# A hybrid retention, attention and RWKV block in float32: RWKV's merge on the preparation's PSUM bank

## The chip, the core and the metric

The kernel runs on one core of one Trainium2 chip. The metric is the device time of one execution in microseconds (us); three executions of the kernel before gave 2938.15, 2952.78 and 2946.3 us, median 2946.3. The engines are named as in the profile: PE is TensorE (matmuls), PEld its weight load, DVE is VectorE, ACT is ScalarE, POOL is GpSimd, SP is SyncE, which issues the DMAs here.

## The reference

Two layers work on 256 latent tokens and 256 context tokens of width 1024. Each layer is half a SwiGLU, a token mixing, and half a SwiGLU. The mixing has three branches that share one input projection: a bidirectional retention, a windowed attention, and a bidirectional RWKV-7. The change touches RWKV alone. For each of its 8 heads (64 wide) and each direction it runs

```
def rwkv7_scan(r, w, k, a, v, kk, s0, reverse):
    '''S_t = S_{t-1} (diag(w_t) - kk_t^T (a_t * kk_t)) + v_t^T k_t ;  y_t = S_t r_t.'''
    def step(S, inp):
        r_t, w_t, k_t, a_t, v_t, kk_t = inp
        sa = -jnp.einsum('bhvk,bhk->bhv', S, kk_t)
        S = (S * w_t[:, :, None, :] + sa[..., None] * (kk_t * a_t)[:, :, None, :]
             + v_t[..., None] * k_t[:, :, None, :])
        return S, jnp.einsum('bhvk,bhk->bhv', S, r_t)
```

over the context from a zero state, and then over the latent tokens from the state that the context left. In the second layer the context's outputs are not wanted, only its states.

## The kernel before, in words

A layer's dense products (`dense`, L346, by way of `mm3`, L185) are split float32: one product is three matmuls (L186, L187, L188) from a high and a low half of the weights and of the activations. Weights stream in by SP (`Weights.get`, L100): a load `raw` (L113), a cast on ACT to `whi` (L114), a subtraction on DVE to `wlo` (L115). In this document a dense matmul means one of these.

RWKV's scan is computed in chunks of 64 tokens, four to a segment (context s = 0, latent s = 1), for a pair of heads p = 0 to 3. Each p has these parts, named by the words of the table `ORDER`:

- `c` (`rw_cols`, L844): r, k and v of the pair, their convolution, the normalised kk.
- `A` and `C` (`rw_prep`, L901, for s = 0 and s = 1), the preparation: decays (L908, L909 and their tanh), scans, the scaled keys `kb`, their transposes `kbT` (L957), the chunk products `gk` and `tg` (L976 and what evacuates them, L980 to L987). All its matmuls go through the PSUM tag `rf`, which has one bank, so each group of matmuls waits until the group before it has been evacuated. At its end the two diagonal 32x32 blocks of each triangular matrix go by DMA through a DRAM tile (L997, L1001) to POOL, which inverts them in 62 instructions (L1008, L1009) and stores the inverse in the DRAM tile `td` (L1012).
- `B` and `D` (`rw_back`, L1146, for s = 0 and s = 1), the back: `rw_merge` (L1015) loads the inverse from `td` into `z` (L1018), transposes it on DVE (L1023) and builds the off-diagonal blocks with 32 small matmuls (L1035, L1040); `rw_vals` (L1045) forms the values `ve` and `vbd` (L1052 to L1060) and, where outputs are wanted, `bv` (L1064); `rw_chain` (L1072) is the walk over the four chunks in both directions, eight steps of L1079, L1081, L1086, L1090 and L1107 with ACT and DVE work between them; `rw_out` (L1117, L1134) normalises the result.

The merge, the values, the walk and the output all go through the PSUM tag `rx`, which has two banks. The walk of `D` starts from the state that the walk of `B` of the same p left.

The order on each engine is not written by hand. The framework's scheduler lays the program out ahead of time with its own estimate of durations: it takes an instruction when what it reads is ready and a home for what it writes is free, and the least urgent dense matmuls fill the places between. So the number of homes of a tag, and which tags share one, set the order on all engines. On the chip each engine then runs its list in that order, whatever the durations turn out to be.

Tags that the change names: `rb` (3 homes) holds the merge's `tn` and `xm`, the walk's `ya` and the output's square; `rt` (8 homes) holds the preparation's temporaries; `ve` (2) the values, `vbd` (one, in the constants' tile `cst`) the values by head; `lo` (3) the low-rank columns of the whole layer.

Of the kernel before, what the change touches and what calls it, by code (L numbers as in the profile page):

```python
# [18 lines left out]
CONSTS = {"ident": 0, "nw": 128, "adab": 176, "ones": 320, "bones": 384, "cm": 512, "mg": 640, "ks": 896, "all": 960}  # L19
# [103 lines left out]
def body(nc, tc, I, O, es, dbg=None):  # L123
# [3 lines left out]
    V, A, G, PE, SP = nc.vector, nc.scalar, nc.gpsimd, nc.tensor, nc.sync  # L127

    def mk(shape, tag, bufs=1, dt=F32):
        return sb.tile(shape, dt, name=tag, tag=tag, bufs=bufs)  # L130
# [3 lines left out]
    def ps(tag):  # L134
        return pp.tile([128, 512], F32, name="ps_" + tag, tag=tag, bufs=NB[tag])
# [13 lines left out]
    def span(S):  # L149
        return slice(S[0] * 256, S[-1] * 256 + 256)  # L150


    cst = mk([128, CONSTS["all"] + 1696 + 4360], "cst")
    n0 = CONSTS["bones"]
    SP.dma_start(out=cst[:, 0:n0], in_=I["cst"][:, 0:n0])
    SP.dma_start(out=cst[:, n0:CONSTS["all"]], in_=I["cst"][:, n0:])
# [1 line left out]
    def const(name, n):  # L158
        return cst[:, CONSTS[name]:CONSTS[name] + n]
# [4 lines left out]
    per = cst[:, CONSTS["all"]:]  # L164
# [3 lines left out]
    def sm(n, key, bufs=8):  # L168

        if key not in rings:  # L170
            rings[key] = [rings["at"], 0, n]
            rings["at"] += n * bufs
            assert rings["at"] <= CONSTS["all"] + 1696 + 4360
        r = rings[key]
        assert r[2] == n
        j = r[0] + n * (r[1] % bufs)
        r[1] += 1
        return cst[:, j:j + n]
# [1 line left out]
    hall = mk([128, KT, 2, 512], "hall", 1, F32R)  # L180
    hs = [(hall[:, kt, 0], hall[:, kt, 1]) for kt in range(KT)]

    rings = {"at": CONSTS["all"] + 1696}

    def mm3(o, w, h, start, stop):  # L185
        PE.matmul(o, w[0], h[0], start=start, stop=False)  # L186
# [19 lines left out]
    st = {"apart": False}  # L206
# [120 lines left out]
    def hl(h, c):  # L327
        return h[0][:, c], h[1][:, c]
# [21 lines left out]
    def first(W, key, H, cs, os, lead=0, lag=0):  # L350

        bl, n = W.take(key), len(os)
        w = {}
        parts = [(0, slice(0, 512))] if lead == 0 else [(0, CS[0]), (lead, CS[1])]
        for i in range(KT + lead + lag):
            for d, part in parts:
                k = i - d
                for j, (o, c) in enumerate(zip(os, cs)):
                    p = slice(max(c.start, part.start), min(c.stop, part.stop))
                    if 0 <= k < KT and p.start < p.stop:  # L360
                        if (k, j) not in w:
                            w[k, j] = W.get(bl[k * n + j])
                        for q in range(2):
                            PE.matmul(o[:, p], w[k, j][q], hl(H[k], p)[0], start=(k == 0 and q == 0 and p.start == c.start), stop=False)  # L364
                k -= lag
                for j, (o, c) in enumerate(zip(os, cs)):
                    p = slice(max(c.start, part.start), min(c.stop, part.stop))
                    if 0 <= k < KT and p.start < p.stop:
                        PE.matmul(o[:, p], w[k, j][0], hl(H[k], p)[1], start=False, stop=(k == KT - 1 and p.stop == c.stop))
# [424 lines left out]
    def conv(o, ct, c, st, dst):  # L794
        w = st["vec"][:, ct * 3:ct * 3 + 3]
        A.activation(dst[:, c], o[:, c], AF.Copy, scale=w[:, 1:2])
        n = (c.stop - c.start) // 256
        d = dst[:, c].rearrange("p (s t) -> p s t", s=n)
        s = o[:, c].rearrange("p (s t) -> p s t", s=n)
        V.scalar_tensor_tensor(d[:, :, 1:256], s[:, :, 0:255], w[:, 0:1], d[:, :, 1:256], ALU.mult, ALU.add)  # L800
        V.scalar_tensor_tensor(d[:, :, 0:255], s[:, :, 1:256], w[:, 2:3], d[:, :, 0:255], ALU.mult, ALU.add)  # L801

    def rw_consts():
        V.memset(per[:, 288:1312], 0.0)
        ub = per[:, 288:800].rearrange("p (d b x) -> p d b x", d=2, b=2)
        return dict(bones=const("bones", 128), cm=const("cm", 128), mg=const("mg", 256).rearrange("p (d x) -> p d x", d=2),
                    one=const("ones", 64), ks=const("ks", 1), ub=[[ub[:, d, b] for b in range(2)] for d in range(2)],
                    vbd=per[:, 800:1312].rearrange("p (q x) -> p q x", q=4))

    def rw_lora(W, H, l, S, st):  # L810
        full = slice(0, 512)
        vec = st["vec"]
        lo = []
        cs, os = (full, full, span(S)), [ps(t) for t in ("mm", "mm", "ap")]
        first(W, "lo", H, cs, os, 1, 1)
        for j, (c, o) in enumerate(zip(cs, os)):
            t = mk([128, 512], "lo", 3)
            conv(o, 12 + j, c, st, t)
            lo.append(t)
        c = span(S)  # L820
        A.activation(lo[0], lo[0], AF.Tanh)
        A.activation(lo[2][:, c], lo[2][:, c], AF.Tanh, scale=0.5)
        V.tensor_scalar(lo[2][:, c], lo[2][:, c], 0.5, 0.5, ALU.mult, ALU.add)
        st["sg"] = lo[2]
        st["lw"] = [[mk([128, 512], "lw", 4, F32R) for d in range(2)] for x in range(2)]
        for x in range(2):
            for d in range(2):
                hs, ot = (slice(64 * y, 64 * y + 64) for y in (d, 1 - d))
                A.copy(st["lw"][x][d][hs], lo[x][hs])
                V.tensor_sub(st["lw"][x][d][ot], lo[x][hs], st["lw"][x][d][hs].bitcast(F32))  # L830
        if l > 0:
            bl = W.take("vd")
            o = ps("mm")
            wh, wl = W.get(bl[0], 2)
            for kt in range(KT):
                ksl = slice(kt * 32, kt * 32 + 32)
                mm3(o[0:32], (wh[:, ksl], wl[:, ksl]), hl(H[kt], full), kt == 0, kt == KT - 1)
            vd = mk([128, 512], "vd")[0:32]
            A.copy(vd, o[0:32])
            st["vd"] = vd  # L840
# [172 lines left out]
        X["td"] = td  # L1013

    def rw_merge(X, st):  # L1015
        z, tn, xm = mk([64, 2, 8, 32], "z", 2), mk([32, 16, 32], "rb", 3)[:, 0:8], mk([64, 16, 32], "rb", 3)[:, 0:8]
        for b in range(2):
            mark = SP.dma_start(out=z[32 * b:32 * b + 32].rearrange("p d u t -> p (d u) t"), in_=X["td"][16 * b:16 * b + 16].rearrange("u j g i -> (j g) u i")).ins  # L1018
        st["marks"].append(mark)
        fl = lambda t: t.rearrange("p u t -> p (u t)")  # L1020
        tg = X["tg"]
        tu = [tg[d].rearrange("p h c t -> p (h c) t") for d in range(2)]
        V.transpose(fl(tn), fl(z[0:32, 0]))  # L1023
        for b in range(2):
            bs = slice(32 * b, 32 * b + 32)
            A.copy(tu[0][bs, :, bs], z[bs, 0])
            V.transpose(tu[1][bs, :, bs], z[bs, 1])

        o = ps("rx")
        ov, o2 = (o[:, j * 256:j * 256 + 256].rearrange("p (u x) -> p u x", x=32) for j in range(2))  # L1030
        ab = (slice(0, 32), slice(32, 64))
        for d in range(2):
            a, b = ab[d], ab[1 - d]
            for u in range(8):
                PE.matmul(ov[b, u], X["off"][a, u], tn[:, u] if d == 0 else z[a, 1, u], start=True, stop=True)  # L1035
        A.copy(xm, ov[0:64])
        for d in range(2):
            a, b = ab[d], ab[1 - d]
            for u in range(8):
                PE.matmul(o2[a, u], xm[b, u], tu[d][b, u, b], start=True, stop=True)  # L1040
        V.tensor_copy(tu[0][ab[0], :, ab[1]], o2[ab[0]])
        A.copy(tu[1][ab[1], :, ab[0]], o2[ab[1]])

    def rw_vals(s, R, st, want_y, X):
        c = CS[s]  # L1045
        v = R["v"]

        ve = [mk([128, 4, 128], "ve", 2) for _ in range(2)]
        vb = st["vbd"]
        o = ps("rx")  # L1050
        for q in range(2):
            PE.matmul(o[:, q * 128:q * 128 + 128], v[:, c.start + q * 128:c.start + q * 128 + 128], st["cm"], start=True, stop=True)  # L1052
        ov = o[:, 0:256].rearrange("p (c d) -> p c d", c=2)
        for a in range(2):
            rows = slice(64 * a, 64 * a + 64)
            for d in range(2):
                A.copy(ve[d][0:64, a::2], ov[rows])
            for h in range(2):
                hs = slice(64 * h, 64 * h + 64)
                A.copy(vb[hs, a::2, hs], ov[rows, :, hs])  # L1060
        X["ve"], X["vb"] = ve, vb
        if want_y:
            o = ps("rx")
            PE.matmul(o[:, 0:256], st["bones"], X["t"][:, 0], start=True, stop=True)  # L1064
            bv = sm(256, "bv", 2)
            V.tensor_tensor(bv, o[:, 0:256], v[:, c], ALU.mult)
            X["bv"] = bv
# [159 lines left out]
    for l in range(2):  # L1227
# [17 lines left out]
        if not RC:  # L1245
            RC.update(rw_consts())
# [120 lines left out]
```

## Time and profile before

| | us |
|---|---|
| median of three runs | 2946.3 |
| the profiled execution | 2950.47 |
| its span, first to last instruction | 2948.7 |
| the mixing of layer 0 (407.8 to 1320) | 912.2 |
| the mixing of layer 1 (2066 to 2758) | 692.0 |
| PE busy in the span | 2797.0 |
| POOL busy in the span | 376.2 |

The profiled execution is 4.2 us over the median of the runs. Busy time is time in which an engine has an instruction under way; a share of it is an average over stages with different limits. In the two mixings RWKV, retention, attention and the dense products are interleaved. The rest of the span is the feed-forward parts, in which the change touches nothing.

### The profile page before, as it was taken

The numbers are of one execution on the slowest core, as the hardware profiler recorded it, in microseconds if no ns is written. First come the engines' busy times: TensorE is split into PE (matmuls) and PEld (weight loads), VectorE is DVE, ScalarE is ACT, GpSimd is POOL, SyncE is SP. The second block draws the span as 40 slices with busy tenths as digits, with TensorE's granted clock in tenths as the row PEclk, the third lists the DMA queues.
The fourth block names the chain that finished last, engine by engine and source line by source line (L and its number), as shares of the span: only waits on it lengthen the run. The fifth ranks groups of instructions, "written<-read, shape, count | busy, mean of one in ns | idle before, by whom it ended". The sixth has DMA issues, their size and how long they took to land. (4 is left out here: it accounts for less than half of the span.)

```text
span 2948.7 us, 47410 instructions
## 1 busy us (share of the span) xinstructions
PE 2797.0 (95%) x16761; PEld 2389.1 (81%) x16761; DVE 2002.5 (68%) x4677; ACT 1319.8 (45%) x2968; POOL 376.2 (13%) x1068
## 2 busy tenths in 40 slices
PE   7999999889999999999999999999989889899999
PEld 6888888767877787788888888888878788788999
DVE  7977668676676666566756466465787767678655
ACT  3322245556555654333223232233567665565544
POOL 0000000522132112000000000000033434330000
PEclk9999999789999999999999999999999888899999
DMA  7655534212333136534534435343433234246554
GB/s 267 232 189 183 163 122 130 83 39 82 111 97 89 49 123 207 176 102 147 195 114 169 147 111 185 104 164 122 137 90 108 75 110 116 61 124 212 170 179 154
DMA packets 259727, 400.97 MB, mean 136 GB/s; under 512 B 78752, under 2 KB 96288, under 8 KB 259488
## 3 DMA queue, kind: packets, MB, share of 16 engines
q1 hardware_dynamic: 259488, 397.93, 42.2%
q8 instruction: 132, 2.16, 0.3%
q14 instruction: 107, 0.88, 0.1%
HBM read 368.33 MB, written 25.82 MB: 134 GB/s over the span
## 5 line engine op out<-in xcount | busy, mean ns | idle before, releaser
L114 ACT CAST whi<-raw 128x512 fp32r<-128x512 f32 x954 | 564.1, 618 | 675.7 <-PE ps_mm L187 350.0
L186 PE MATMUL ps_mm<-hall,whi 128*128 128x512 f32 (+1 forms) x2320 | 845.1, 365 | 10.2 <-DVE rr_v L801 4.0
L188 PE MATMUL ps_mm<-hall,wlo 128*128 128x512 f32 (+1 forms) x2320 | 842.6, 364 | 2.0 <-DVE wlo L115 2.0
L187 PE MATMUL ps_mm<-hall,whi 128*128 128x512 f32 (+1 forms) x2320 | 840.8, 363 | 0.0
L115 DVE TENSOR_TENSOR wlo<-raw,whi 128x512 fp32r<-128x512 f32 x954 | 643.8, 691 | 104.3 <-ACT whi L114 68.3
L186 PEld LDWEIGHTS ps_mm<-hall,whi 128*128 128x128 f32 x2320 | 442.9, 191 | 80.6 <-ACT cst L981 4.4
L188 PEld LDWEIGHTS ps_mm<-hall,wlo 128*128 128x128 f32 x2320 | 441.6, 191 | 74.8 <-DVE wlo L115 4.1
L187 PEld LDWEIGHTS ps_mm<-hall,whi 128*128 128x128 f32 x2320 | 442.0, 191 | 71.4 <-issue 0.2
L186 PE MATMUL ps_mm<-hid,whi 128*128 128x512 f32 (+1 forms) x737 | 260.6, 354 | 0.0
L187 PE MATMUL ps_mm<-hid,whi 128*128 128x512 f32 (+1 forms) x737 | 259.9, 354 | 0.0
L188 PE MATMUL ps_mm<-hid,wlo 128*128 128x512 f32 (+1 forms) x737 | 257.3, 354 | 0.0
L1008 POOL TENSOR_TENSOR cst<-acc,cst 128x60 f32<-128x60 f32 (+24 forms) x496 | 172.4, 348 | 615.5 <-DMA acc<-ad__10934 59.2
L401 DVE TENSOR_TENSOR ft<-ft,ps_mm 128x512 f32<-128x512 f32 (+1 forms) x80 | 49.7, 621 | 210.4 <-PE ps_mm L188 198.1
L373 DVE SCALAR_TENSOR_TENSOR x<-ps_mm,cst,x 128x256 f32<-128x256 f32 x136 | 61.0, 480 | 193.1 <-PE ps_mm L188 193.1
L853 POOL TENSOR_TENSOR ll<-lora,lh 128x512 fp32r<-128x512 f32 x8 | 10.3, 1282 | 1359.2 <-DVE ft L300 942.6
L1009 POOL TENSOR_TENSOR cst<-cst 128x60 f32<-128x60 f32 (+24 forms) x496 | 176.2, 355 | 38.1
L236 DVE SCALAR_TENSOR_TENSOR ft<-m,cd 128x1024 bf16<-128x1024 f32 x136 | 163.0, 1221 | 9.8 <-DMA m<-ada 9.8
L237 DVE SCALAR_TENSOR_TENSOR m<-m,cd 128x1024 f32<-128x1024 f32 x136 | 165.4, 1221 | 0.7
L186 PEld LDWEIGHTS ps_mm<-hid,whi 128*128 128x128 f32 x737 | 139.1, 189 | 19.6
L187 PEld LDWEIGHTS ps_mm<-hid,whi 128*128 128x128 f32 x737 | 139.1, 189 | 19.4
L188 PEld LDWEIGHTS ps_mm<-hid,wlo 128*128 128x128 f32 x737 | 138.5, 189 | 19.4
L187 PE MATMUL ps_mm<-wlo,hall 128*128 128x256 f32 x416 | 122.6, 295 | 2.7 <-DVE wlo L115 2.6
(339 smaller groups left out, 4505.3 us busy)
## 6 DMA issues: line engine op xcount, KB each, us to landing
m<-ada SPq DMA_DIRECT2D x136, 512.0 KB, 4.4
raw<-w0b SPq DMA_DIRECT2D x214, 256.0 KB, 2.9
raw<-w1b SPq DMA_DIRECT2D x211, 256.0 KB, 3.2
raw<-w0a SPq DMA_DIRECT2D x132, 256.0 KB, 2.8
raw<-w0c SPq DMA_DIRECT2D x132, 256.0 KB, 4.5
raw<-w1a SPq DMA_DIRECT2D x132, 256.0 KB, 4.3
raw<-w1c SPq DMA_DIRECT2D x132, 256.0 KB, 3.9
gd<-ft SPq DMA_DIRECT2D x24, 256.0 KB, 2.0
```

What stands on the lines that cost most here:

```text
L114: nc.scalar.copy(hi, raw)
L115: nc.vector.tensor_sub(lo, raw, hi.bitcast(F32))
L186: PE.matmul(o, w[0], h[0], start=start, stop=False)
L187: PE.matmul(o, w[0], h[1], start=False, stop=False)
L188: PE.matmul(o, w[1], h[0], start=False, stop=stop)
L236: V.scalar_tensor_tensor(junk, raw, 1.0, st["cond"][0], ALU.mult, ALU.mult, accum_out=md[:, kt, 0:1])
L237: V.scalar_tensor_tensor(raw, raw, 1.0, st["cond"][1], ALU.mult, ALU.mult, accum_out=md[:, kt, 1:2])
L373: V.scalar_tensor_tensor(xs[n][:, CS[s]], o[:, CS[s]], gate[:, n, s:s + 1], xs[n][:, CS[s]], ALU.mult, ALU.add)
L401: V.tensor_tensor(sg[:, c], sg[:, c], pu[:, c], ALU.mult)
L853: G.tensor_sub(ll, lw, lh.bitcast(F32))
L1008: G.tensor_tensor(w, acc[j // 16][:, j % 16, j + 1:32].unsqueeze(1).to_broadcast([128, m, n]), tt[:, 0:m, j:j + 1].to_broadcast([128, m, n ...
L1009: G.tensor_tensor(tt[:, 0:m, j + 1:32], tt[:, 0:m, j + 1:32], w, ALU.add)
```

## The change

Four things move. The merge's product tile `o` is taken from `rf` (the preparation's one bank) and no longer from `rx` (the walk's two). The merge's tiles `tn` and `xm` are taken from `rt` (8 homes) and no longer from `rb`. `vbd` has a home for each segment, and its zeros cost one more memset. `ve` has four homes, which it shares with the first two low-rank columns; the third keeps `lo`, with one home. The number and the shapes of the matmuls stay as they were.

```
-    cst = mk([128, CONSTS["all"] + 1696 + 4360], "cst")
+    cst = mk([128, CONSTS["all"] + 2208 + 4360], "cst")
...
     def rw_consts():
         V.memset(per[:, 288:1312], 0.0)
+        V.memset(per[:, 1696:2208], 0.0)
...
-                    vbd=per[:, 800:1312].rearrange("p (q x) -> p q x", q=4))
+                    vbd=[per[:, a:a + 512].rearrange("p (q x) -> p q x", q=4) for a in (800, 1696)])
...
-            t = mk([128, 512], "lo", 3)
+            t = mk([128, 512], "ve", 4) if j < 2 else mk([128, 512], "lo")
...
     def rw_merge(X, st):
-        z, tn, xm = mk([64, 2, 8, 32], "z", 2), mk([32, 16, 32], "rb", 3)[:, 0:8], mk([64, 16, 32], "rb", 3)[:, 0:8]
+        z, tn, xm = mk([64, 2, 8, 32], "z", 2), mk([32, 16, 32], "rt", 8)[:, 0:8], mk([64, 16, 32], "rt", 8)[:, 0:8]
...
-        o = ps("rx")
+        o = ps("rf")
...
-        ve = [mk([128, 4, 128], "ve", 2) for _ in range(2)]
-        vb = st["vbd"]
+        ve = [mk([128, 4, 128], "ve", 4) for _ in range(2)]
+        vb = st["vbd"][s]
```

The scheduler lays the program out anew from these, so the order changes on every engine from the first mixing on. In the listings below, lines of the changed kernel stand one higher than before (L1036 is the merge's L1035, L958 the transposes of L957, L977 the products of L976), and equal instructions that follow each other share a row.

PE, layer 1, head pair 1: the preparation's transposes into `ps_rf` (`A1`) in the kernel before. `ps_mm` is a dense product, L1040 a merge.

```order
L1052 MATMUL ps_rx<-cst,rr_v 128x128 x2
L186 MATMUL ps_mm<-whi,hall 128x256
L187 MATMUL ps_mm<-wlo,hall 128x256
L957 MATMUL ps_rf<-cst,kb 128x128 x2
L1040 MATMUL ps_rx<-tg,rb 32x32 x16
L957 MATMUL ps_rf<-cst,kb 128x128 x2
L188 MATMUL ps_mm<-whi,hall 128x256
```

The same preparation in the changed kernel, among steps of the walk `D0` (L1080 to L1108) and retention's scores (L548, L549).

```order
L958 MATMUL ps_rf<-cst,kb 128x128 x4
L548 MATMUL ps_sc<-rqh,rks 128x256
L549 MATMUL ps_sc<-rql,rks 128x256
L958 MATMUL ps_rf<-cst,kb 128x128 x4
L1108 MATMUL ps_rx<-ve,tg 64x64 x4
L977 MATMUL ps_rf<-arz,kb 128x2x64 x2
L1080 MATMUL ps_rx<-cst,gk 128x128
L1082 MATMUL ps_rx<-cst,ar 128x128
L1080 MATMUL ps_rx<-cst,gk 128x128
L1082 MATMUL ps_rx<-cst,ar 128x128
L573 MATMUL ps_po<-cst,ft 128x128 x2
```

The transposes stood among dense matmuls that did not depend on them; now they stand in a stretch without dense matmuls, and the merge of the pair before has moved ahead of the whole preparation.

PE, layer 0, the last merge (`D3`) in the kernel before: L1134 and L1135 are the output of the walk `B3`.

```order
L188 MATMUL ps_mm<-ro,wlo 128x512
L1134 MATMUL ps_rx<-cst,rb 128x64 x4
L1135 MATMUL ps_rx<-lo,cst 128x256
L1035 MATMUL ps_rx<-rb,cst 32x32 x8
L1035 MATMUL ps_rx<-z,cst 32x32 x8
L186 MATMUL ps_mm<-ro,whi 128x512
```

The same merge in the changed kernel, L1036 and L1041, between the L1087 and the L1091 of one step of the walk `B3`.

```order
L1087 MATMUL ps_rx<-cst,tg 64x64 x2
L1036 MATMUL ps_rf<-rt,cst 32x32 x8
L1036 MATMUL ps_rf<-z,cst 32x32 x8
L1087 MATMUL ps_rx<-cst,tg 64x64 x2
L1091 MATMUL ps_rx<-ve,kbT 128x128
L1041 MATMUL ps_rf<-tg,rt 32x32 x16
L186 MATMUL ps_mm<-ro,whi 128x512 x2
L1108 MATMUL ps_rx<-ve,tg 64x64 x2
```

The merge stood directly behind the output of the walk before; now it stands inside that walk, and the rest of the walk is queued behind it.

## Rows read from the trace of the kernel before

**Rows 1.** The page: span, and busy us (share of the span) xinstructions by engine.

```profile
span 2948.7 us, 47410 instructions
PE 2797.0 (95%) x16761; PEld 2389.1 (81%) x16761; DVE 2002.5 (68%) x4677; ACT 1319.8 (45%) x2968; POOL 376.2 (13%) x1068
```

**Rows 2.** Windows: stretch, us, busy (xcount) by engine, granted clock, DMA share, GB/s.

```profile
407.80:1320.00 912.20, 850.07 (x5197) 706.59 (x5196) 624.64 (x1650) 470.05 (x1140) 183.84 (x532) 0.95 0.35 107
1320.00:2066.00 746.00, 740.49 (x3532) 616.97 (x3531) 454.86 (x846) 223.32 (x396) 0.00 (x0) 0.99 0.43 144
2066.00:2758.00 692.00, 626.73 (x4705) 554.52 (x4705) 513.15 (x1385) 415.74 (x1044) 192.15 (x532) 0.92 0.39 116
```

**Rows 3.** Groups on PE: busy us, mean ns | idle us before them <- releaser.

```profile
L976 PE MATMUL ps_rf<-arz,kb 128*128 128x256 f32 (+1 forms) x256 | 69.3, 398 | 2.0 <-DVE tg L987 1.4 <-DVE gk L984 0.3 <-ACT cst L1095 0.3
L1086 PE MATMUL ps_rx<-cst,tg 64*64 64x64 f32 x512 | 54.8, 236 | 6.5 <-ACT cst L1083 6.4
L1079 PE MATMUL ps_rx<-cst,gk 128*128 128x128 f32 (+1 forms) x256 | 54.7, 299 | 12.6 <-DVE cst L1102 6.1 <-DVE rb L1113 5.0 <-ACT tg L1042 0.7
L1090 PE MATMUL ps_rx<-ve,kbT 128*128 128x128 f32 x224 | 44.4, 300 | 3.2 <-ACT ve L1088 2.8
L1107 PE MATMUL ps_rx<-ve,tg 64*64 64x64 f32 x384 | 42.0, 237 | 12.9 <-ACT ve L1088 8.3 <-DVE cst L1102 4.3
L957 PE MATMUL ps_rf<-cst,kb 128*128 128x128 f32 x128 | 24.3, 315 | 9.2 <-DVE kb L946 6.2 <-ACT kbT L958 3.1
L1052 PE MATMUL ps_rx<-cst,rr_v 128*128 128x128 f32 x64 | 13.1, 335 | 2.8 <-ACT kbT L958 2.8
L1035 PE MATMUL ps_rx<-rb,cst 32*32 32x32 f32 x256 | 12.0, 199 | 10.4 <-DVE rb L1023 10.3
L1134 PE MATMUL ps_rx<-cst,rb 64*128 64x64 f32 x48 | 5.6, 238 | 5.7 <-DVE rb L1131 5.7
```

**Rows 4.** Timeline of PE, the first merge: start us, us, instruction, [idle before].

```profile
548.42 0.28 PE L186 MATMUL ps_mm<-whi,hall 128*128 128x256 f32 x1
548.54 0.28 PE L187 MATMUL ps_mm<-wlo,hall 128*128 128x256 f32 x1
...
549.48 1.03 PE L976 MATMUL ps_rf<-arz,kb 128*128 128x256 f32 x4
558.08 0.90 PE L1035 MATMUL ps_rx<-rb,cst 32*32 32x32 f32 x13 [7.57 <-DVE rb L1023]
...
568.16 0.42 PE L187 MATMUL ps_mm<-wlo,hall 128*128 128x256 f32 x1
568.38 0.41 PE L188 MATMUL ps_mm<-whi,hall 128*128 128x256 f32 x1
```

**Rows 5.** Windows, behind that wait.

```profile
553.30:577.10 23.80, 18.42 (x129) 16.91 (x130) 12.43 (x51) 10.04 (x33) 8.01 (x25) 0.50 0.36 98
```

**Rows 6.** Timeline, from the preparation C3 of layer 1 to its merge.

```profile
2606.75 1.03 PE L976 MATMUL ps_rf<-arz,kb 128*128 128x256 f32 x4
...
2616.91 0.24 POOL L1008 TENSOR_TENSOR cst<-acc,cst 128x31 f32<-128x31 f32 x1 [31.75 <-DMA acc<-ad__25540]
...
2644.22 2.54 SPq L1012 DMA_DIRECT2D td<-cst  x4
...
2648.17 0.88 SPq L1018 DMA_DIRECT2D z<-td  x2
...
2652.06 0.59 PE L1035 MATMUL ps_rx<-rb,cst 32*32 32x32 f32 x13
```

**Rows 7.** Timeline of PE, from the preparation C2 of layer 0 to its merge.

```profile
913.61 1.02 PE L976 MATMUL ps_rf<-arz,kb 128*128 128x256 f32 x4
...
995.63 0.46 PE L1134 MATMUL ps_rx<-cst,rb 64*128 64x64 f32 x4
996.65 0.68 PE L1035 MATMUL ps_rx<-rb,cst 32*32 32x32 f32 x13
```

**Rows 8.** Groups on DVE, the memset of the constants.

```profile
L804 DVE MEMSET cst<- 128x1024 f32 x1 | 0.9, 912 | 1.0 <-PEq L1359 1.0
```

More of the change, by code (lines that the diff above doesn't have):

```diff
@@ L172, in sm @@
             rings["at"] += n * bufs
-            assert rings["at"] <= CONSTS["all"] + 1696 + 4360
+            assert rings["at"] <= CONSTS["all"] + 2208 + 4360
         r = rings[key]
@@ L181, in body @@
     hs = [(hall[:, kt, 0], hall[:, kt, 1]) for kt in range(KT)]
-    rings = {"at": CONSTS["all"] + 1696}
+    rings = {"at": CONSTS["all"] + 2208}
     def mm3(o, w, h, start, stop):
```

## The prediction

> **What bounds the kernel now.** I read the page's busy times first: PE is busy 2797.0 of 2948.7 us [rows 1], so a change that leaves PE's work alone can win or lose only where PE stands idle or runs slowly. Then the windows by stage: the feed-forward stretch between the two mixings is busy 740.5 of 746.0 us at a granted clock of 0.99, while the mixings are busy 850.1 of 912.2 and 626.7 of 692.0 at 0.95 and 0.92 [rows 2]. The mixings hold 62.1 + 65.3 = 127.4 us of idle, and of clock 0.05 of 912.2 and 0.08 of 692.0, about 101 us more. Every term below is a share of these.
>
> Then the groups on PE, for what it waits for there. The RWKV groups wait 10.4 us at the merge (L1035), 9.2 + 2.0 = 11.2 in the preparation (L957, L976), 2.8 at the values (L1052), 6.5 + 12.6 + 3.2 + 12.9 = 35.2 in the walk (L1086, L1079, L1090, L1107) and 5.7 at the output (L1134) [rows 3], 65.3 together. The releasers are ACT and DVE, the engines between two dependent groups of matmuls, and none is a bank that comes free late.
>
> The timeline shows what one such wait is. PE issues its list in order: after the first preparation's last L976 it stood 7.57 us before the first merge, with dense matmuls queued behind it [rows 4]. Behind that wait the granted clock was 0.50 for 23.8 us [rows 5], the lower level, 1.2 GHz: dense matmuls of 256 columns that had started 0.12 us apart now started 0.22 apart [rows 4].
>
> Last, the latency under that wait. From the end of a preparation's last L976 (2606.75 + 1.03) to its merge (2652.06) 44.3 us passed [rows 6]: DMAs to POOL's tiles until 2616.91, POOL's 62 instructions until the store at 2644.22, the load of `z`, the transpose. In the six pairs in which the merge came soonest it took 43 to 49 us. So a merge that stands less than about 43 us of PE work behind its preparation makes PE wait, unless other waits on the way fill the time.
>
> **The change part by part.** No matmul is added or removed and no shape changes. What is added is one memset of 128x512 on DVE: the one of 128x1024 took 0.912 us at the program's start, while the inputs were still on their way [rows 8], so this is some 0.46 us, hidden; at worst 0.46. More homes for `ve` and `vbd` let the values be formed ahead of the merge; nothing waits for that by itself, so nothing by itself, and what it gives the walk is in the walk's term. `tn` and `xm` in `rt` take two of eight homes for the few us of a merge; the bound is one wait of the preparation's size, already in its term.
>
> What costs is the order. The merge now takes turns with the preparation in the one bank of `rf`, and the scheduler has moved the preparations late: the transposes of layer 1's A1, which stood among dense matmuls, now stand in a stretch without any, together with the walk of D0. And the merge is no longer behind the previous output but inside the previous walk, as with D3 of layer 0, where the rest of that walk is queued behind it.
>
> How much shorter the cover has become I counted over both built orders. For each pair of dependent groups on PE I added up the PE instructions that stand between them, each at its median distance from start to start in this trace (0.12 us for a dense matmul of 256 columns [rows 4], twice that for 512), and took what is missing to the latency that the same kind of pair has in this trace, taken at the shortest tenth of its pairs (43.3 us from preparation to merge). What is missing in all pairs, before and now:
>
> - preparation to merge: 66 and 88 us (nine short merges of sixteen before, ten now);
> - within the preparation: 33 and 67;
> - values and merge to the walk's first use: 8.3 and 29.6;
> - within the walk: 43.4 and 47.6;
> - walk to output: 13.1 and 18.1.
>
> These are not times, since pairs overlap: 66 us missing at the merges went with 10.4 us of idle there. So I scale each measured idle time with its count. The merge gains 10.4 x 0.33 = 3.5 us, the preparation 11.2 x 1.03 = 11.5, the values 2.8 x 2.57 = 7.2, the walk 35.2 x 0.10 = 3.4, the output 5.7 x 0.38 = 2.2: 27.8 us. With each latency at its shortest pair and not at the shortest tenth the growth is 0.36, 0.91, 3.41, -0.40 and 1.04, and the sum 3.7 + 10.2 + 9.6 - 13.9 + 5.9 = 15.5 us. I take 22 us, between the two. The walk is the term on which they differ: its true bound is -14 to +3.4.
>
> The clock is the unknown. In the mixings 127.4 us of idle went with 101 us of clock, 0.79 us for each, so 22 us more idle may bring 0 to 17 us. I take 0: the wait that cost most, 7.57 us with 23.8 us at 1.2 GHz behind it, is at the first merge, and there the cover grows from 31.0 to 36.6 us, so that wait loses about 5.6 us and part of its slow stretch. SP's queue moves with the merges (the store to `td` and the load of `z`, behind which weight loads wait); the number of transfers is the same, and I put it at nothing, with one wait of the merge's size, 7.6 us, as the worst.
>
> The sum is 2950.5 (the profiled execution) + 22 = 2972.5. That execution is 4.2 us above the median of the runs, so 2968 us is forecast for the median.
>
> **The rivals.** A difference below 0.5%, some 15 us, can't be told from none here.
>
> *The banks were the brake (faster).* C2's merge in layer 0 began 82.0 us after the end of its preparation, one us behind the previous walk's output L1134 [rows 7], where 44 us would have done; ten of the sixteen merges came more than 53 us behind theirs. With the merge off the walk's two banks, and the values formed early, a walk can begin where the last one ends. Then the walk's idle falls by its bound, 14 us, the first merge's by 5.6, and the preparation's growth is hidden by other work: 20 us less, 2926 us. Against it: the waits in rows 3 name ACT and DVE, and the counts say that the preparation, in one bank, is what becomes late. It decides once the walk's idle falls by more than the preparation's grows, 11 us. The Trainium skill's Perfetto Trace Analysis, Optimization Strategy, would read it this way: the same gap repeating on the engine that should be saturated can mean that SBUF or PSUM has no room for the next tile. By that rule the two banks of `rx` and the two homes of `ve` are the cause, and the result is this rival's; but the rule says as much of the one bank of `rf`, which this change loads further, and no row here names a bank.
>
> *The waits only move (no change).* A merge needs its 44 us wherever PE stands during them; a wait taken earlier in a walk makes a later one shorter, PE's work is the same 2797 us, and the two mixings end with the same dense products behind the last walk. Then 2946, within 15 us either way. For it: the idle at the merges is 10.4 us though 66 are missing. Against it: all five counts grow.
>
> *The clock follows the idle (much slower).* The forecast's 27.8 us of idle, with 0.79 us of clock for each, give 50 us: 2996. For it: the one long wait in rows 4 and 5. Against it: most single waits in rows 3 are short, and the longest one shrinks.
>
> That the change does not do what it says is excluded: in the built order the merge writes `ps_rf`.
>
> **How the numbers follow.** The forecast gets 0.35 (2955 to 2985), the banks 0.27, no change 0.20, the clock 0.18. The forecast's low end, 0.05, and 0.02 of the banks lie within 0.5%. So slower 0.30 + 0.18 = 0.48, within 0.5% 0.20 + 0.05 + 0.02 = 0.27, faster 0.25. The predicted time is 2968 us. The range must reach into the banks' case and the clock's: 2922 to 3004.
>
> **What would show it.** Right: PE's idle at L957 and L976 together rises from 11.2 to about 20 us, at the values and the walk's first step by some 7, and at the merge to about 14; the window of layer 1 grows more than that of layer 0, since A1's preparation there has lost its dense matmuls; the granted clock of the two mixings stays near 0.95 and 0.92. Wrong: the walk's 35.2 us fall to near 20 and the merges begin 45 us after their preparations everywhere, which is the banks' case; or the idle of the five groups stays near 65 us in sum, which is no change; or the granted clock of a mixing falls by 0.02 or more, which is the clock's case. If the idle falls on L114's casts or on weights instead, the order of SP's queue was the cause, and the argument here missed it.

## The result: 1.1% slower

| | median, us | runs |
|---|---|---|
| before | 2947.78 | 4 (2938.15 to 2952.78) |
| after | 2977.91 | 4 (2975.64 to 2983.01) |

The ratio is 1.0109, 95% interval 1.0079 to 1.0138: 30 us slower. The profiled execution took 2977.34 us, against 2950.47 before.

The page of the changed kernel, to be read against [rows 1]:

```profile
span 2975.6 us, 47454 instructions
PE 2805.0 (94%) x16761; PEld 2399.0 (81%) x16761; DVE 1992.9 (67%) x4678; ACT 1307.3 (44%) x2968; POOL 378.0 (13%) x1068
```

The span grew by 26.9 us. PE's idle time, span less busy, grew from 151.7 to 170.6 us, by 18.9; PE's busy time grew by 8.0 at the same number of matmuls, while the granted clock of the whole span fell from 0.963 to 0.958. Windows of the changed kernel, cut where PE's counts match those of [rows 2] to within four (stretch, us, PE busy and count, granted clock, DMA share, GB/s):

```profile
406.50:1325.00 918.50, 857.21 (x5201) 0.93 0.34 105
1325.00:2072.00 747.00, 739.86 (x3531) 1.00 0.44 146
2072.00:2786.30 714.30, 629.52 (x4705) 0.91 0.40 117
```

The mixing of layer 0 is 6.3 us longer and that of layer 1 22.3 us; the feed-forward stretch grew by 1.0, and before and behind these 2.7 us were won. In layer 1 the idle time went from 65.3 to 84.8 us. In layer 0 it fell a little, from 62.1 to 61.3; what grew there is the busy time, by 7.1 us, at a granted clock of 0.93 where it was 0.95 [rows 2]. Groups on PE, as in [rows 3], with three of other branches:

```profile
L977 PE MATMUL ps_rf<-arz,kb 128*128 128x256 f32 (+1 forms) x256 | 65.5, 379 | 2.2 <-ACT arz L973 1.2 <-DVE tg L988 0.4 <-ACT ft L565 0.3
L1087 PE MATMUL ps_rx<-cst,tg 64*64 64x64 f32 x512 | 57.5, 239 | 13.0 <-ACT cst L1084 11.9 <-DVE tg L1042 1.1
L559 PE MATMUL ps_po<-ft 128*128 128x128 f32 x320 | 55.9, 309 | 20.6 <-DVE ft L556 19.7 <-DVE ft L554 0.8
L1080 PE MATMUL ps_rx<-cst,gk 128*128 128x128 f32 (+1 forms) x256 | 55.7, 304 | 5.8 <-ACT cst L1061 3.5 <-DVE rb L1111 0.9 <-DVE rb L1114 0.6
L1091 PE MATMUL ps_rx<-ve,kbT 128*128 128x128 f32 x224 | 47.2, 311 | 9.9 <-ACT ve L1089 9.5
L1108 PE MATMUL ps_rx<-ve,tg 64*64 64x64 f32 x384 | 42.4, 238 | 8.6 <-DVE cst L1103 4.1 <-ACT ve L1089 3.1 <-ACT cst L1101 0.8
L548 PE MATMUL ps_sc<-rqh,rks 128*128 128x256 f32 (+1 forms) x64 | 26.4, 413 | 4.8 <-DVE rks L537 4.6
L958 PE MATMUL ps_rf<-cst,kb 128*128 128x128 f32 x128 | 23.3, 309 | 11.0 <-DVE kb L947 7.6 <-ACT whi L114 1.8 <-ACT kbT L959 1.4
L1036 PE MATMUL ps_rf<-rt,cst 32*32 32x32 f32 x256 | 12.8, 206 | 11.0 <-DVE rt L1024 8.8 <-DVE tg L988 2.3
L1053 PE MATMUL ps_rx<-cst,rr_v 128*128 128x128 f32 x64 | 11.3, 306 | 0.0
L1135 PE MATMUL ps_rx<-cst,rb 64*128 64x64 f32 x48 | 6.1, 256 | 7.6 <-DVE rb L1132 7.5
```

By these names almost nothing happened in RWKV. Its five groups wait 69.1 us against 65.3: the walk 37.3 against 35.2, the preparation 13.2 against 11.2, the merge 11.0 against 10.4, the output 7.6 against 5.7, the values 0.0 against 2.8. The largest growth has retention's name: L559 waits 20.6 us, where it waited 9.3 before:

```profile
L559 PE MATMUL ps_po<-ft 128*128 128x128 f32 x320 | 52.0, 295 | 9.3 <-DVE ft L556 7.4 <-DVE ft L554 1.5
```

The timeline shows what stands behind the name. The first merge, the place of [rows 4], first on PE:

```profile
550.56 1.02 PE L977 MATMUL ps_rf<-arz,kb 128*128 128x256 f32 x4
557.99 1.22 PE L559 MATMUL ps_po<-ft 128*128 128x128 f32 x4 [6.41 <-DVE ft L556]
558.87 0.56 PE L548 MATMUL ps_sc<-rqh,rks 128*128 128x256 f32 x1
559.23 0.41 PE L549 MATMUL ps_sc<-rql,rks 128*128 128x256 f32 x1
559.57 0.90 PE L1036 MATMUL ps_rf<-rt,cst 32*32 32x32 f32 x13
```

The same place on ACT, and then on DVE:

```profile
553.73 0.86 ACT L1027 COPY tg<-z 32x256 f32<-32x256 f32 x2 [8.07 <-DMA z<-td]
```

```profile
553.73 0.90 DVE L1028 STREAM_TRANSPOSE tg<-z 32x256 f32<-32x256 f32 x2 [5.24 <-DMA z<-td]
...
556.12 0.85 DVE L985 TENSOR_TENSOR gk<-ps_rf,cst 64x256 f32<-64x256 f32 x2
...
557.51 0.42 DVE L556 TENSOR_TENSOR ft<-ps_sc,dt 128x256 f32<-128x256 f32 x1
```

DVE and ACT take their lists in order too. The merge's copies out of `z` (L1024 and L1028 on DVE, L1027 on ACT) stood at the head of both lists until the inverse had come back from POOL, and retention's `ft` stood behind them on DVE. PE waited for `ft`, and the profile names `ft`; what was late is `z`. So I read this wait as the merge's of [rows 4], 6.41 us where it was 7.57, under another name. Of the 6.41 us, 2.15 passed before `z` was there (553.73); in the other 4.26 DVE worked off what had queued up behind it, `ft` among the last.

It repeats in layer 1. ACT of the changed kernel at the merge of head pair 1, and PE there:

```profile
2393.69 0.26 ACT L1089 COPY ve<-ps_rx 64x128 f32<-64x128 f32 x1 [1.45 <-PE ps_rx L1087]
2403.10 0.40 ACT L1027 COPY tg<-z 32x256 f32<-32x256 f32 x1 [9.15 <-DMA z<-td]
2403.53 0.26 ACT L1089 COPY ve<-ps_rx 64x128 f32<-64x128 f32 x1
```

```profile
2397.70 0.28 PE L186 MATMUL ps_mm<-hall,whi 128*128 128x256 f32 x1
2403.84 0.80 PE L1091 MATMUL ps_rx<-ve,kbT 128*128 128x128 f32 x2 [5.87 <-ACT ve L1089]
```

The walk's second copy of `ve` takes 0.26 us, but it stood behind 9.15 us of waiting for `z`. The profile puts the 5.87 us down to the walk. The waits at 2208.18 (4.68 us, L559), 2537.19 (5.48, L1087) and 2637.41 (4.46, L188) are of this kind too, the first of them least clearly, since it ended 3.8 us after `z` had come. What DVE, and then ACT, waited for `z` in the changed kernel (total, times, longest us):

```profile
DVE tg L1028 <- DMA z<-td: 35.3, 11, 7.1
DVE rt L1024 <- DMA z<-td: 33.1, 6, 8.8
```

```profile
ACT tg L1027 <- DMA z<-td: 72.6, 18, 9.2
```

The same before:

```profile
DVE tg L1027 <- DMA z<-td: 38.3, 9, 7.0
DVE rb L1023 <- DMA z<-td: 12.7, 5, 7.4
```

```profile
ACT tg L1026 <- DMA z<-td: 61.7, 19, 10.7
```

To see what of it reaches PE I added up, from the trace, each idle time of PE that overlaps a wait of DVE or ACT for `z` (of more than 0.3 us) and ended with that wait or at most 5 us after it: 25.9 us before, 42.7 after. The growth is 16.8 us, where all idle time grew by 18.9. This sum is rough: it takes each idle time whole, and only 17.8 us of it before and 25.4 after lie within the waits for `z` themselves; with at most 3 us in place of 5 it is 25.9 and 31.6. Nor do the two growths match by layer: in layer 0 the sum rises by 6.2 us where all idle time fell by 0.8, in layer 1 by 10.5 of 19.5.

The other rows have their answers. The stretch of [rows 5] has a granted clock of 0.64 now, not 0.50:

```profile
553.30:577.10 23.80, 18.53 (x152) 0.64 0.38 109
```

From C3 of layer 1 to its merge 45.0 us passed (2649.00 to 2694.00), 44.3 in [rows 6], and from C2 of layer 0 59.4 us in place of the 82.0 of [rows 7] (951.48 to 1010.92). The added memset took 0.485 us, where 0.46 had been put down from [rows 8]:

```profile
L805 DVE MEMSET cst<- x1: 485/485/485, 2.0 to 2.0; 128x512 f32 x1
```

### The profile page after: what moved, and what is told of

Read it like the earlier page. It is cut to its first block, busy times and chain, and to the rows that moved or that the text cites. A ratio compares the mean times of both kernels' runs of the same rounds, so it can differ in the third digit from the quotient of the medians.

```text
span 2975.6 us, 47454 instructions
## 1 busy us (share of the span) xinstructions
PE 2805.0 (94%) x16761; PEld 2399.0 (81%) x16761; DVE 1992.9 (67%) x4678; ACT 1307.3 (44%) x2968; POOL 378.0 (13%) x1068
## 4 chain that ended last, share of the span: by engine, by line
PE 57%; POOL 5%; DVE 5%; DMA 3%; ACT 3%; issue 2%; SPq 1%; DVEq 0%; POOLq 0%; ACTq 0%
PE ps_mm L186 15%; PE ps_mm L187 15%; PE ps_mm L188 15%; POOL cst L1010 2%; POOL cst L1009 2%; PE ps_rx L1087 1%; DVE wlo L115 1%; PE ps_mm L364 1%; DMA z<-td 1%; PE ps_rx L1080 1%; PE ps_rx L1108 1%; PE ps_rx L1091 1%; PE ps_rf L977 1%; PE ps_po L776 1%; DMA td<-cst 1%
## 5 line engine op out<-in xcount | busy, mean ns | idle before, releaser
L188 PE MATMUL ps_mm<-hall,wlo 128*128 128x512 f32 (+1 forms) x2320 | 844.4, 365 | 5.5 <-DVE wlo L115 5.5
L114 ACT CAST whi<-raw 128x512 fp32r<-128x512 f32 x954 | 557.3, 616 | 277.8 <-PE ps_mm L187 147.0
L188 PEld LDWEIGHTS ps_mm<-hall,wlo 128*128 128x128 f32 x2320 | 441.3, 190 | 76.0 <-DVE wlo L115 7.1
L188 PE MATMUL ps_mm<-hid,wlo 128*128 128x512 f32 (+1 forms) x737 | 257.3, 354 | 0.0
L854 POOL TENSOR_TENSOR ll<-lora,lh 128x512 fp32r<-128x512 f32 x8 | 10.4, 1304 | 1353.3 <-ACT lh L853 940.7
L210 ACT CAST hid<-ft 128x512 fp32r<-128x512 f32 (+1 forms) x88 | 49.9, 568 | 263.5 <-DVE ft L401 263.5
L188 PEld LDWEIGHTS ps_mm<-hid,wlo 128*128 128x128 f32 x737 | 138.5, 189 | 19.4
```

What stands on the lines that cost most here:

```text
L114: nc.scalar.copy(hi, raw)
L188: PE.matmul(o, w[1], h[0], start=False, stop=stop)
L210: A.copy(dst[0], src)
```

## The experiments

Each kernel was timed beside the kernel before on the same chip. The three sets of four ran on three chips (the kernel before took 2949.1, 2949.85 and 2949.43 us there), so kernels of different sets are compared by their ratios. "Cover" is the forecast by the prediction's rule, with the latencies at the shortest tenth: what is missing to cover each group, before and in that kernel, scaled on the idle times of [rows 3]. The expectations of x5 to x12 give the plain sum of the counts; the cover of these eight in the table at the end stands in no expectation.

**x1_bank**, the bank alone.

```
-        o = ps("rx")
+        o = ps("rf")
```

> The kernel before with one part of the change alone: the merge's product tile in the preparation's bank (rf), its temporaries in rb and the values' homes as before. Theory (cover): the loss of the whole change (30 us) comes from the new order that the shared bank forces; in this built order the short cover between dependent matmuls sums to 267 us against 164 before and 251 in the whole change, which scaled on the idle times of before gives 23 to 39 us: 2971 to 2987 us for a before of 2948. Rival (tiles): the bank alone is worth less than 8 us and the loss sits with tn and xm in rt. Rival (reshuffle): any new order of this kernel lands within 20 us of before on either side, and the count says nothing about which.

2989.92 us, ratio 1.0135 (1.0119 to 1.015): the bank alone costs at least as much as the whole change (1.0109, 1.0079 to 1.0138; the intervals overlap). Groups on PE of x1, then the waits of DVE:

```profile
L559 PE MATMUL ps_po<-ft 128*128 128x128 f32 x320 | 57.9, 321 | 29.5 <-DVE ft L556 20.4 <-DVE ft L554 8.6
...
L957 PE MATMUL ps_rf<-cst,kb 128*128 128x128 f32 x128 | 23.3, 312 | 21.1 <-DVE kb L946 18.3 <-ACT kbT L958 1.9 <-DVE cst L764 0.8
```

```profile
DVE rb L1023 <- DMA z<-td: 41.4, 10, 9.7
```

Here the preparation's transposes do wait, 21.1 us against 9.2, and DVE's first reader of `z` waits 41.4 us against 12.7.

**x2_tiles**, the merge's tiles alone.

```
-... tn, xm = mk([32, 16, 32], "rb", 3)[:, 0:8], mk([64, 16, 32], "rb", 3)[:, 0:8]
+... tn, xm = mk([32, 16, 32], "rt", 8)[:, 0:8], mk([64, 16, 32], "rt", 8)[:, 0:8]
```

> The kernel before with another part alone: the merge's tn and xm in rt, the product tile in rx and the values' homes as before. Theory (cover): the count of short cover in this built order is 241 us against 164, scaled 28 to 30 us: 2976 to 2978 us for a before of 2948, so the tiles alone cost as much as the whole change. Theory of the prediction (bank): the bank is the cause, so this stays within 8 us of before. Rival (reshuffle): anywhere within 20 us of before, on either side.

2978.3 us, 1.0104 (1.0073 to 1.0135). The tiles alone cost as much as the whole change, though no bank is shared.

**x3_homes**, the homes of `ve` and `vbd` alone (and the memset).

```
-        V.memset(per[:, 288:1312], 0.0)
+        V.memset(per[:, 288:1312], 0.0); V.memset(per[:, 1696:2208], 0.0)
...
-            t = mk([128, 512], "lo", 3)
+            t = mk([128, 512], "ve", 4) if j < 2 else mk([128, 512], "lo")
...
-        vb = st["vbd"]
+        vb = st["vbd"][s]
```

> The kernel before with the values' part alone: vbd with a home for each segment and its memset, ve with four homes that it shares with two low-rank columns; the merge as before. Theory (cover): the count falls from 164 to 160 us, scaled -6 to -4 us: 2942 to 2944 us for a before of 2948, that is no change. Rival (banks were the brake): the values formed early are worth 10 us or more. Rival (reshuffle): anywhere within 20 us of before.

2940.45 us, 0.9965 (0.9954 to 0.9976), faster than both kernels. Of the two edits I take `vbd`'s second home to be the one, since with the `ve` and `lo` edits alone PE's order came out as that of the kernel before; no run here tests it. Bank, tiles and homes come to +40, +31 and -10 us by their ratios, 61 in sum, twice what the three bring together; so the costs don't add, and the bank and the tiles look like two ways to one cost (x12 below).

**x4_null**, two independent lines exchanged.

```
-        A.activation(kk, k, AF.Copy, scale=kks)
         A.activation(sq, k, AF.Square, scale=kks)
+        A.activation(kk, k, AF.Copy, scale=kks)
```

> A change that means nothing: in rw_cols the two independent ACT instructions that form kk and its square are written in the other order, nothing else; the scheduler lays out most of the mixing anew from it (8592 lines of difference on PE). Theory (cover): the count is 152 us against 164, scaled -11 to -2 us: 2937 to 2946 us for a before of 2948. Rival (reshuffle): a new order by itself moves the time by 10 to 20 us, on either side; then 30 us of the change can't be ascribed to a bank.

2950.1 us, 1.0003 (0.9994 to 1.0012). It moves thousands of rows in PE's order and costs nothing; the 10 to 20 us of the rival did not come, and the time lies 4 us above the cover's range. One other order is not all orders: without any sharing, x6 and x8 below move the time by -13 and +9 us. But no kernel that shares nothing comes near the 30 us of the change.

**x5_after_words**, the changed kernel with words of `ORDER` moved (shown for layer 1).

```
-... kv B0 D0 c1 A1 H1 ... c2 D1 H2 A2 H3 ... B2 H5 D2 G7 A3 C3 G8 ...
+... kv B0 c1 A1 D0 H1 ... c2 H2 A2 D1 H3 ... B2 H5 G7 A3 D2 C3 G8 ...
```

> The changed kernel whole, with five words of the table ORDER moved so that each preparation stands ahead of the merge of the pair before it (A1 ahead of D0, A2 ahead of D1, C2 ahead of B2, and in the second layer A3 ahead of D2). Theory (a shared bank or tag is handed out in the program's order, so with the merge of D0 written ahead of A1 the preparation A1 has to wait for that merge, and with the words moved it need not): the loss goes, 2940 to 2962 us; the count of missing cover falls from 251 to 176 (before: 164). Rival 1 (the one bank and its buffers are too scarce, in whatever order they are handed out): the time stays at 2970 to 2985. Rival 2 (the table of words was tuned, and any other order costs): 2990 or more.

2979.61 us, 1.0096 (1.0079 to 1.0113). The theory that the turn in the program does it has fallen. The merge's own wait did shrink (L1036 3.2 us) and so did the first reader's on DVE, but PE waits elsewhere:

```profile
L559 PE MATMUL ps_po<-ft 128*128 128x128 f32 x320 | 55.9, 310 | 18.4 <-DVE ft L556 17.3 <-DVE ae L783 0.5 <-ACT rt L981 0.4
...
L548 PE MATMUL ps_sc<-rqh,rks 128*128 128x256 f32 (+1 forms) x64 | 26.9, 421 | 7.6 <-DVE rks L537 6.7 <-DVE rb L1111 0.8
...
L787 PE MATMUL ps_ap<-cst,ae 128*128 128x128 f32 x24 | 4.9, 318 | 7.8 <-DVE ae L783 7.8
```

**x6_before_words**, the same words in the kernel before, as a control.

> The kernel before with the same five words of ORDER moved, and nothing else: the control of x5_after_words. In the kernel before the merge shares nothing with the preparation, so the theory expects no change: 2940 to 2956 us (count 165 against 164). If the words by themselves are worth something, this shows it: below 2935, they are a gain of their own that x5 must be measured against; above 2965, the old place of the words was worth something.

2935.39 us, 0.9955 (0.9939 to 0.997): a gain of its own that I had not expected, and the shortest time of all. So with the words moved the change costs 44 us, more than without. This fastest kernel waits longest at its merges by name, 20.7 us where the kernel before waits 10.4 and x5 3.2:

```profile
L1035 PE MATMUL ps_rx<-rb,cst 32*32 32x32 f32 x256 | 12.4, 202 | 20.7 <-DVE rb L1023 20.7
```

**x7_tiles_words**, x2 with the same words.

> x2_tiles (only tn and xm of the merge in the preparation's tag rt, 2978) with the five words of ORDER moved. Theory: the tag is handed out in the program's order as the bank is, so the loss of x2 goes: 2935 to 2955 us (count 150, the merges 37 and the preparation 33). Rival (the merge's tiles crowd the preparation out of its buffers): it stays above 2965.

2973.44 us, 1.0077 (1.0063 to 1.009): the loss of x2 stays. Here it has the walk's name:

```profile
L1086 PE MATMUL ps_rx<-cst,tg 64*64 64x64 f32 x512 | 58.6, 246 | 19.7 <-ACT cst L1083 19.5
...
L1107 PE MATMUL ps_rx<-ve,tg 64*64 64x64 f32 x384 | 44.4, 245 | 13.2 <-DVE cst L1102 13.0
```

**x8_tiles_own**, the merge's tiles in a tag of their own.

```
-... tn, xm = mk([32, 16, 32], "rb", 3)[:, 0:8], mk([64, 16, 32], "rb", 3)[:, 0:8]
+... tn, xm = mk([32, 16, 32], "mt", 2)[:, 0:8], mk([64, 16, 32], "mt", 2)[:, 0:8]
```

> The kernel before with tn and xm of the merge in a tag of their own with two homes, shared with nobody, the words of ORDER as before. Theory: what cost in x2_tiles was the sharing with the preparation and not the leaving of rb, so this is no loss: 2940 to 2956 us (count 168 against 164). Rival (a merge that no longer waits for the output before it in rb is let go too early, and PE waits in it): 2965 to 2985, as x2_tiles.

2958.22 us, 1.003 (1.0019 to 1.0042), just over the theory's range. Of the 31 us of x2 some 22 come from the tag being the preparation's, 9 from leaving `rb`.

**x9_one_pair**, the changed kernel with the sharing for one pair only (`rw_merge` takes tag and bank as an argument).

```
-        rw_merge(X[s], st)
+        rw_merge(X[s], st, (("rt", 8), "rf") if l == 1 and p == 2 else (("rb", 3), "rx"))
```

> The changed kernel with the merge's tiles and bank shared with the preparation for one pair only, p = 2 of the second layer; the other seven pairs have the merge in rx and rb as in the kernel before, the homes of the values stay as changed (so x3_homes, 2940, is what it stands against). New theory (the sharing makes the preparations slip behind the merges, and what costs is that the last one, C3 of the second layer, ends with fewer dense matmuls left): C3 ends after 8739 dense matmuls here, as in the changed kernel, x1 and x2, against 8619 in the kernel before, x3 and x4; from dense matmul 8578 to the end of the mixing the kernels with 8739 lost 15 to 25 us, those with 8619 lost 0 to 4. So this one pair costs 15 to 25 us over x3: 2955 to 2966. Rival (the loss is spread over all sixteen merges, as the count of missing cover has it, 180 against 251 in the changed kernel and 160 in x3): 4 to 9 us over x3, 2944 to 2950.

2945.92 us, 1.0001 (0.9989 to 1.0014). The time lies in the rival's range; over x3 it is 10.6 us by the ratios (0.0036 of 2949, give or take 5 us by the intervals), between the theory's 15 to 25 and the rival's 4 to 9. One pair of eight thus costs about a quarter of the 42 us that separate the changed kernel from x3. The theory of the last preparation is not borne out: C3 ends as late as in the changed kernel, and most of the loss did not come.

**x10_last_pair**, the sharing for `p == 3` only.

> The changed kernel with the sharing only for the last pair, p = 3, of both layers, behind which no preparation stands; the others as in the kernel before, the homes as changed. New theory: no preparation can slip, so little is lost: C3 of the second layer ends after 8687 dense matmuls (x6 with 8687 lost 15 us in the tail, x8 with 8699 lost 8), so 0 to 12 us over x3_homes: 2940 to 2953. Rival (a merge in the preparation's bank costs wherever it stands): a quarter of the merges and more of what the tail loses, 2955 or more.

2936.58 us, 0.9966 (0.9949 to 0.9983), as x3: where no preparation stands behind the merge, the shared bank and tag cost nothing. That refutes the rival that a merge in the preparation's bank costs wherever it stands.

**x11_homes_words**, x3 with the words of x6.

> Only the homes of the values (x3, 9 us faster than before) with the five words of ORDER moved (x6, 14 us faster): nothing is shared with the preparation. C3 of the second layer ends after 8619 dense matmuls, so the tail loses nothing: 2920 to 2935 us if the two add up. Rival (the count of missing cover, 178 against 164): 2945 to 2955.

2945.57 us, 0.9987 (0.997 to 1.0005), in the rival's range: the two gains do not add up, and with the words moved the homes lose 9.5 us by the ratios (x11 against x6).

**x12_no_bank**, the changed kernel without the bank.

```
-        o = ps("rf")
+        o = ps("rx")
```

> The changed kernel without the bank: tiles in rt, homes of the values as changed, the merge's product in rx. If tiles and bank each bring the whole loss, since either one already ties the preparation to the merge, this is x2_tiles (2978) with the homes' gain: 2965 to 2980. Rival (the bank brings the changed kernel's loss and the tiles little within it): 2945 to 2955. C3 of the second layer ends after 8739 dense matmuls, which speaks for the first.

2972.12 us, 1.0087 (1.0066 to 1.0108), as expected of x2 with the homes' gain. Without the bank the loss is as good as whole.

All together, in the order of the cover's forecast (us; measured is the ratio less one, times 2949; the last column is PE's idle behind `z`, added up as above, from one profiled execution of each):

| kernel | merge shares with the preparation | cover | measured | PE behind `z` |
|---|---|---|---|---|
| before | no | 0 | 0 | 25.9 |
| x3 | no | -4.2 | -10.3 | 19.2 |
| x4 | no | -2.2 | +0.9 | 23.8 |
| x6 | no | +0.3 | -13.3 | 28.1 |
| x10 | last pair | +0.6 | -10.0 | 22.9 |
| x8 | no | +3.4 | +8.8 | 32.7 |
| x11 | no | +4.4 | -3.8 | 19.9 |
| x9 | one pair | +6.0 | +0.3 | 21.7 |
| x7 | all, tag | +10.4 | +22.7 | 29.3 |
| x5 | all, both | +23.5 | +28.3 | 32.3 |
| x12 | all, tag | +26.8 | +25.7 | 42.2 |
| after | all, both | +27.9 | +32.1 | 42.7 |
| x2 | all, tag | +29.9 | +30.7 | 34.4 |
| x1 | all, bank | +38.8 | +39.8 | 52.3 |

Six kernels share for all sixteen merges and lie at +23 to +40; eight share for none or a few and lie at -13 to +9. The two columns of the cover and the measurement differ by 7.2 us in the mean square over the thirteen changed kernels (correlation 0.93). That is no proof of the count, for the sharing alone does as well: with one mean for the six (+29.9 us) and one for the seven changed kernels that share for none or a few (-3.9), 6.5 us are left over (0.93). Within the six the cover still goes with the time (0.90), within the seven much less (0.46). For five kernels (x1 to x4 and the changed one) a forecast with each latency at its shortest pair is on record too: it is 12 us off, and the one with the shortest tenth 4.

The last column goes with the time as well (0.85), but not in size: x2 and x7 have 8.5 and 3.4 us more behind `z` than the kernel before and are 31 and 23 us slower, while x8 has 6.8 more and is 9 slower. What is shown is that sharing with the preparation costs; that the wait for `z` is how it costs is shown in part.

## Why the prediction was right in size, and where it was wrong

**That it is slower, and where.** Right: the order costs, by way of what merge and preparation share, and layer 1 grows more (22.3 us against 6.3). x1, x2 and x12 show that either sharing is enough, x4 that one other order is not, x10 that it costs nothing where no preparation follows. The text had both in one sentence and priced the tiles inside the preparation's term; that the tiles alone bring the whole loss it had not said. The reason it gave for layer 1, that A1's preparation has lost its dense matmuls, is not where the wait is. A1's transposes before (between 2240 and 2290 us), and in the changed kernel (2212 to 2314 us):

```profile
L957 PE MATMUL ps_rf<-cst,kb 128*128 128x128 f32 x8 | 1.4, 279 | 0.0
```

```profile
L958 PE MATMUL ps_rf<-cst,kb 128*128 128x128 f32 x8 | 2.1, 420 | 0.0
```

They ran longer, 420 ns each where it was 279, and waited 0.0 us in both.

**The five terms.** This is the step that failed: "So I scale each measured idle time with its count." It gave +3.5 for the merge, +11.5 for the preparation, +7.2 for the values, +3.4 for the walk and +2.2 for the output; by name they measured +0.6, +2.0, -2.8, +2.1 and +1.9, a sum of 3.8 us against 27.8. The text itself had named five groups near 65 us as the sign of no change, and they stand at 69.1 in a kernel that is 1.1% slower. What failed is the reading of names: 10.4 us at L1035 was taken for what the merges cost, but DVE and ACT wait for `z` ahead of whatever stands behind it in their lists, and by the sum above some 25.9 us stood behind `z` already before, as 7.57 us at L1035 [rows 4] and as waits of the walk and of a dense matmul. In the terms' place the runs showed two things. Sharing the bank or the tag costs +23 to +40 us as one whole, and not a part for each group. And in the changed kernel the idle time behind `z` grew by up to 16.8 us, over four times the 3.8 of the five names; that it is the only term is not shown, since it accounts for about half of what layer 1 gained in idle time, and for 8.5 of 31 us in x2 and 3.4 of 23 us in x7.

**The choice of 22 us.** The rule gave 27.8 and 15.5, and I took the middle. So 2968 us was forecast and 2978 measured, within the range. The sum of idle and clock came out at 26.9 us in the profiled execution and 30 in the medians, and in the table the first of the two choices holds over twelve other kernels, as the sharing alone does. For this kernel the size is in part luck: 18.9 us of idle time where 22 were put down, but at other waits than the five, and 8.0 us of busy time where none was. Why a sum fits whose parts don't: the cover that is missing is real, but PE pays for it at whichever wait ends last. That is how I read it; the table shows the sum alone.

**The clock.** Taken as 0, bounds 0 to 17: measured 8.0, which is 0.42 us for each us of idle and not 0.79. No fixed price shows: against the kernel before, x1 has 35.5 us more idle time and 1.1 us less busy time, x10 18.3 us less idle time and 11.2 us more busy time. The text's sign of the clock's case was a mixing whose clock falls by 0.02. Layer 0 comes near it, 0.95 to 0.93 in the windows and 0.946 to 0.935 with one digit more, and its 6.3 us are busy time; but the 50 us of that case did not come. The first merge's wait was to lose 5.6 us and lost 1.2; its stretch gained clock all the same.

**Homes, memset, SP.** The memset was hidden. "Nothing" for the homes was 10 us too little of a gain, as x3 has it; with the words moved they lose (x11). The waits on weights grew (L188 in the dense products of `hall` from 2.0 to 5.5 us), but 4.46 us of that, at 2637.41, ended 1.9 us after ACT's wait of 5.89 us for `z` (to 2635.53), and I put them down to it and not to SP's queue.

**The rivals.** The banks were no brake of any size: the walk waits 37.3 us against 35.2, and leaving its banks is the dearest part (x1). But the text's reading that none of the waits in [rows 3] is a bank that comes free late is wrong. L1113 is the last to read a step's bank of `rx`, and L1079 takes the next free one: 5.0 us of its 12.6 are a wait for a bank, and so are the 3.1 us of L957 for L958, which empties `rf`. In the changed kernel L1080 waits 1.5 us for such readers (L1111 and L1114), so some of that did go, and the walk waited elsewhere. The waits did move, as the second rival had it, but they also grew.

**What stays open.** In x5 and x7 the words put the merge and the preparation in the same turn as in x6, and 44 and 38 us separate them from it (44.2 and 34.3 in the profiled executions). By the table only 4.2 and 1.2 us of that lie behind `z`; 15.9 and 10.4 us are more busy time of PE at the same matmuls, and the rest is idle time, spread over retention, attention and dense products in x5, and in the walk in x7. Why sharing costs there too was not settled. And of x9's 10 us it wasn't tried which of the two merges brings them.

One sentence of the text ahead needs mending. It says that the number of homes of a tag sets the order, and which tags share one. Of the two it is the second that the runs show: x2 and x8 differ in whether the merge's tiles share the preparation's tag, and x2, though it has eight homes there against two, is the slower by some 22 us. That more homes leave the order as it is (ten for `rt` in x2, four for `rb` before) I saw in built orders alone; no run here shows it.

## What to carry to other kernels

A wait on a busy in-order engine is paid by whoever is queued behind it, so before a term is priced by its name, follow the release one step further: what was that engine itself waiting for? Two parts with a long latency between them (here 44 us through POOL) are best given no buffer in common; eight homes did not help here (x2). And when several edits act through one order, their costs don't add, and each is worth a kernel of its own: the part of this change that helps by itself (x3, 0.9965) was hidden under the one that hurts.

## What was not expected of the hardware

The way from a preparation to its merge was put at 43 us and more; C3 of layer 0 in the changed kernel took 37.0 (L977 ends at 1109.32, L1036 starts at 1146.36). And behind a little shorter wait, 6.41 us in place of 7.57, the granted clock was much higher, 0.64 in place of 0.50 over the same 23.8 us, in which PE ran 152 matmuls in place of 129 [rows 5]; in the changed kernel dense matmuls were back at 0.12 us from 572.8 us on.
